# Stick-breaking attention: value products of two units together, projection steps dealt three and one, odd scores in the transposes' banks

## The chip, the core and the metric

The kernel runs on one core of a Trainium2 chip. The time is the device time of one execution, in microseconds (us). The engines work through instruction queues of their own and wait for each other through semaphores: PE does the matmuls (its weight loads are listed apart as PEld), ACT activations and casts, DVE elementwise work and scans, POOL a little elementwise work, SP issues the DMAs. PSUM, into which matmuls write, has eight banks; a tile of 128 x 512 fp32 fills one.

## The reference

A trunk of two layers: a recurrent block, an FFN, a stick-breaking attention and another FFN, on 1024 tokens of 1024 channels. The change is in the attention:

```python
def stick_breaking_attention(x, w_qkv, w_o):
    bsz, seq, _ = x.shape
    qkv = jnp.einsum("bsd,de->bse", x, w_qkv).reshape(bsz, seq, 3, N_HEADS, HEAD_DIM)
...
    scale = 1.0 / math.sqrt(HEAD_DIM)
    outs = []
    for blk in range(seq // Q_BLOCK):
        t0 = blk * Q_BLOCK
        t1 = t0 + Q_BLOCK
        qb = q[:, :, t0:t1]
        kb = k[:, :, :t1]
        vb = v[:, :, :t1]
        z = jnp.einsum("bhqd,bhkd->bhqk", qb, kb).astype(jnp.float32) * scale
...
        strict = s_idx < t_idx
        log_fail = jnp.where(strict, jax.nn.log_sigmoid(-z), 0.0)
        suffix = lax.cumsum(log_fail, axis=3, reverse=True) - log_fail
        weights = jnp.where(strict, jnp.exp(jax.nn.log_sigmoid(z) + suffix), 0.0)
        outs.append(jnp.einsum("bhqk,bhkd->bhqd", weights.astype(vb.dtype), vb))
...
    return jnp.einsum("bse,ed->bsd", o, w_o)
```

There are 16 heads of 64 channels and query blocks of 128.

## The kernel before

Matrices that need fp32 accuracy are kept as a high and a low part, and a product is three matmuls (mm3, L142: high x high, high x low, low x high). Heads are treated in eight pairs, q = 0 to 7, with hx = 0 or 1 for the head within its pair; LAST (L1700) is pair 7.

The attention runs as one loop of steps u, from -10 to 191 (L1915), in an order that is written out by hand (manual_schedule): on each engine the instructions run in the order in which the Python code issues them. A step mixes several streams of work:

- A **score chunk** (chunk_list, L1681). Each head has 12: eight on the diagonal (j = 0 to 7, 256 to 512 keys wide) and four off it (j = 4 to 7, 512 wide). z_part (L1686) does two matmuls into a bank of the pool psZ, which has two banks; z_rest (L1708) is ACT's sigmoid of it into SBUF; scan (L1730) is DVE's scan along the keys. One step later turn_weights (L1742) casts the result to fp16 (ACT), takes the rest (DVE, L1751) and has SP transpose both by DMA into tiles T. Chunks run ten steps ahead of the value products.
- A **unit of value products** (unit_list, L1762). Each head has 12: group G = 0 has key blocks 0 to 3, group G = 1 has 4 to 7 and then 0 to 3. av_part (L1785) does two fp16 matmuls (four for the first two blocks of the diagonal) that add into one bank of psO; with the last block of a group the result goes to ACT and DVE.
- **Projection steps** ("fill", qkv_steps, L1571): each is one mm3 of 512 columns towards q, k and v of the next pair, in psQ (two banks). Eight make a group; after the last one evacuate (L1600) copies the result out in two halves: the first is issued at once, the second when the next projection step is called. The start of a projection also issues the load of raw weights (load_link, L1523) and queues the split of the next weights.
- **Queued pieces**: `later` gives one piece a step (splitting weights, gathering results, the norms' squares and sums, column_norms L1530), `due` runs what was set for this step (copies and transposes of q, k and v by SP and ACT), and one or two loads (`back`) bring stored results back to SBUF.

For the last pair the weights are not turned by DMA: t_part (L1766) transposes them on PE into psT (two banks, used for nothing else) and t_split (L1775) casts and splits them on ACT and DVE; the products of unit u+2 and u+3 are prepared at an even step u. As projections run out, out_fill (L1857) begins the output projection (tiles ob and ob_ps). Before the change each even step calls its own av_part, ahead of the projection steps (or, from the last pair on, ahead of the transposes), and each odd step calls its own at its end; two projection steps follow in each:

```python
                if u % 2 == 0 and 0 <= u < last_two - 2:
                    av_part(*units[u])
...
                if u >= -2:
                    for _ in range(2):
                        next(fill, None)
...
                if u % 2 and u >= 0:
                    av_part(*units[u])
```

In the trace the scores are z_ps, the value products av_ps, the projections qk_ps, the PE transposes wt_ps, the norms' sums n_ps.

Of the kernel before, what the change touches and what calls it, by code (L numbers as in the profile page):

```python
# [8 lines left out]
F32 = mybir.dt.float32  # L9
# [8 lines left out]
P = 128  # L18
# [4 lines left out]
NB = 512  # L23
# [11 lines left out]
def trunk(  # L35
# [166 lines left out]
    def stats(acc, ps_pool, tag, n, i0=0, i1=4):  # L202
        ps = ps_pool.tile([P, NB], F32, tag=tag, name="st_ps")
        accs = acc if isinstance(acc, tuple) else (acc,)
        for i in range(i0, i1):
            for a in accs:
                nc.tensor.matmul(
                    ps[:, i : i + 1], lhsT=a[:, i * P : (i + 1) * P], rhs=ones, start=a is accs[0], stop=a is accs[-1]
                )
        rstd(rcol[:, 4 * n + i0 : 4 * n + i1], ps[:, i0:i1])  # L210
# [49 lines left out]
    with ExitStack() as st, tc.manual_schedule(engines={E.PE, E.Activation, E.DVE, E.Pool, E.SP}):  # L260
# [49 lines left out]
        ps = pst("vps0")  # L310
# [71 lines left out]
        for r0, r1 in ((0, 32), (32, 64), (64, P)):  # L382
            ps = pst("vps")
# [1088 lines left out]
    NP = HEADS // 2  # L1472
# [15 lines left out]
    with ExitStack() as st:  # L1488
# [3 lines left out]
        psZ = pos.enter_context(tc.tile_pool(name="psZ", bufs=2, space=PSUM, side="right", reuse_waits="tile"))  # L1492
        psT = st.enter_context(tc.tile_pool(name="psT", bufs=2, space=PSUM, reuse_waits="tile"))
# [26 lines left out]
        def stage(task, steps=1):  # L1520
            soon.append([steps, task])

        def load_link(i):  # L1523
            q, which = divmod(i, 3)
            if q < NP:
                raws[i] = load_raw(cols(w_qkv, which * D + q * P), (ND,))
            else:
                mix[0].load(which)

        def column_norms(raw, q):  # L1530
            sq = ap.tile([P, ND, P], BF16, tag="vx", name="sq", bufs=2)
            r3 = raw.rearrange("p (k c) -> p k c", k=ND)

            def sums():
                n_ps = psZ.tile([P, NB], F32, tag="z", name="n_ps")[:, 0:1]
                for k in range(ND):
                    nc.tensor.matmul(
                        n_ps, lhsT=sq[:, k], rhs=g2[:, k : k + 1], start=k == 0, stop=k == ND - 1
                    )

                n2, h = (ap.tile([P, 1], t, tag=x, name=x, bufs=2) for x, t in (("n2", F32), ("nh", I32)))
                sv[q], av_[q] = (ap.tile([P, 1], I32, tag=x, name=x, bufs=3) for x in ("sv", "av"))
                nc.vector.tensor_scalar(n2, n_ps, 1e-30, 2.0, op0=ALU.max, op1=ALU.mult)
                one = float(1 << 23)
                nc.vector.tensor_single_scalar(h, n2.bitcast(I32), 24, op=ALU.logical_shift_right)

                def factors():
                    nc.gpsimd.tensor_scalar(sv[q], h, -one, 213 * one, op0=ALU.mult, op1=ALU.add)
                    nc.gpsimd.tensor_scalar(av_[q], h, one, 41 * one, op0=ALU.mult, op1=ALU.add)

                stage(factors, 2)

            squared = lambda i: nc.scalar.square(sq[:, 4 * i : 4 * i + 4], r3[:, 4 * i : 4 * i + 4])
            return lambda: squared(0), lambda: squared(1), sums
# [123 lines left out]

        W = {}

        def chunk_list(q, hx):  # L1681
            cut = lambda j: (j + 1) * P - (NB if j >= 4 else 0)
            diag = [(q, hx, j, j // 4, j // 4 * NB, j // 4 * NB + max(cut(j), 256), True) for j in range(NT)]
            return diag + [(q, hx, j, 0, 0, NB, False) for j in range(4, NT)]

        def z_part(q, hx, j, ci, c0, c1, diag):  # L1686
            nk = (j + 1) * P
            ps = psZ.tile([P, NB], F32, tag="z", name="z_ps")
            lhsT = Q[q][hx][:, j * P : (j + 1) * P]
            nc.tensor.matmul(ps[:, 0 : c1 - c0], lhsT=lhsT, rhs=KK[q][hx][:, 0, c0:c1], start=True, stop=False)  # L1690
            nc.tensor.matmul(ps[:, 0 : c1 - c0], lhsT=lhsT, rhs=KK[q][hx][:, 1, c0:c1], start=False, stop=True)  # L1691
            return ps
# [1 line left out]

        LAST = NP - 1  # L1700

        def stay(key, shape, tag):
            if key not in W:
# [4 lines left out]
        def z_rest(ps, q, hx, j, ci, c0, c1, diag):  # L1708
            n = min(c1, (j + 1) * P) - c0
            if q == LAST:  # L1710
                if not diag:
# [28 lines left out]
        T = {}  # L1740

        def turn_weights(q, hx, j, ci, c0, c1, diag):  # L1742
            paired = diag and j % 4 < 2
            if q == LAST or paired and j % 4 == 0:
                return
# [16 lines left out]
        def unit_list(q, hx):  # L1762
            kbs = ((0, 1, 2, 3), (4, 5, 6, 7, 0, 1, 2, 3))
            return [(q, hx, G, kb, kb == 4 * G, kb == 3) for G in range(2) for kb in kbs[G]]
# [20 lines left out]
        def av_part(q, hx, G, kb, first, last):  # L1785
# [5 lines left out]
            parts_ = []  # L1791
            if q == LAST:
                parts_ = [(q0, NB, t[:, q0:].rearrange("p (j c) -> p j c", c=P)) for t in ready.pop((hx, G, kb))]
# [53 lines left out]
        units = [u for q, hx in heads for u in unit_list(q, hx)]  # L1847
# [27 lines left out]
        with tc.manual_schedule(engines={E.PE, E.Activation, E.DVE, E.Pool, E.SP}):  # L1875


            load_link(1)
            first = qkv_steps(0)
            between = {  # L1880
                12: lambda: stats(rbc[0], psO, "o", 0),
                16: lambda: stats(rbc[1], psO, "o", 1),
                18: lambda: nc.gpsimd.tensor_scalar_mul(rs, rcol, -SC),
                22: lambda: broadcast_r(psO, "o", 0),
                25: lambda: broadcast_r(psO, "o", 1),
            }
            def due():
                now = soon[:]
                soon.clear()
                for steps, task in now:  # L1890
                    if steps > 1:
                        stage(task, steps - 1)
                    else:
                        task()

            for i in range(1, 2 * ND * NH + 3 + AHEAD):
                next(first)
                if i in between:
                    between[i]()
                due()  # L1900
                if i > 4 and later:
                    later.pop(0)()

            gains = [len(units) - x for x in (31, 29, 27)]

            last_two, out_work = len(units) - 2 * 12, out_fill()
            amount = {x: 2 for x in (9, 10, 11, 12)}
            amount.update({x: 1 for x in (*range(-5, 1), *range(14, 21))})
            c = 0

            def turn(some):
                for a in some:
                    turn_weights(*a)

            for u in range(-LEAD, len(units)):  # L1915
                some = chunks[c : c + 1]
                c += 1
                if u < -2:
                    for _ in range(2):
                        next(fill, None)  # L1920
                due()
                for _ in range(2 if u >= last_two - 8 and u % 2 == 0 else 1):
                    if back:
                        nc.sync.dma_start(*back.pop(0))
                for a in some:
                    z_rest(z_part(*a), *a)
                if u % 2 == 0 and u + 2 >= last_two:
                    av_part(*units[u])
                    two = [(x, t_part(*x)) for x in units[u + 2 : u + 4]]
                    for x, tp in two:  # L1930
                        ready[x[1:4]] = t_split(tp, *x)
                for a in some:
                    scan(*a)
                now, turning = turning, list(some)
                turn(now)
                if u % 2 == 0 and 0 <= u < last_two - 2:
                    av_part(*units[u])
                if u - last_two == 9:
                    mix[0].w[mix[0].order[1]] = next_weights(mix[0].raw.pop(1), nc.gpsimd)
                if later:  # L1940
                    later.pop(0)()
                if u >= -2:
                    for _ in range(2):
                        next(fill, None)
                for _ in range(amount.get(u - last_two, 0)):
                    next(out_work)
                if u in gains:
                    z_rest(z_part(*chunks[c]), *chunks[c])
                    scan(*chunks[c])
                    turning.append(chunks[c])  # L1950
                    c += 1
                if u % 2 and u >= 0:
                    av_part(*units[u])
            while later or soon:
                due()
                if later:
                    later.pop(0)()
# [46 lines left out]
```

## Time and profile before

| | us |
|---|---|
| median of 3 runs | 2114.78 (2114.1 to 2115.55) |
| profiled execution, its own time | 2114.74 |
| its span, first to last instruction | 2112.9 |
| first and last start of a score matmul in it | 989.9 and 1374.6 |
| first and last start of a value product | 1006.3 and 1392.4 |

A row of a group names line, engine, operation and tiles (out<-in), then the shape and the count; a row of a timeline gives the start in us, the duration, and in brackets how long the engine was idle before and what released it. Rows of waits read: who waited, for whom, us in all, times, the longest. Matmul records start when the matmul is taken up and their ends are modelled, so that neighbours overlap. PEclk is the share of the full TensorE clock that was granted.

### The profile page before, as it was taken

What the parts mean: (1) busy time and instruction counts of PE and PEld (TensorE: products, weight loads), DVE (VectorE), ACT (ScalarE), POOL (GpSimd) and SP (SyncE); (2) the same over time, 40 slices, a digit from 0 to 9 for tenths busy, and PEclk for the clock granted to TensorE, in tenths of its full rate; (3) what the DMA queues carried; (4) which work ended last, traced back from release to release, by engine and by line L of the source; (5) the groups of instructions that cost most, each with busy time, mean ns of one, the idle gap of its engine ahead of it and who ended that gap; (6) DMA issues with size and microseconds to landing.
All of it is one profiled execution on the core that took longest, in us unless ns stands there. A gap on an engine that the chain in (4) does not pass through costs nothing.

```text
span 2112.9 us, 27977 instructions
## 1 busy us (share of the span) xinstructions
PE 2096.9 (99%) x10022; PEld 1720.7 (81%) x10022; DVE 1771.3 (84%) x2579; ACT 1184.6 (56%) x1906; POOL 139.1 (7%) x118
## 2 busy tenths in 40 slices
PE   8999999999999999999999999999999999999998
PEld 7888888888888888888777777678888888888887
DVE  6888768888888788796999999968888888888886
ACT  6567535444444445466778878744544444454456
POOL 1222010000000000000011111011000000000002
PEclk9999999999999999999999999999999999999999
DMA  7111431334434776434888888952224444686452
GB/s 241 50 45 45 144 105 50 110 120 145 162 129 158 244 256 199 147 118 100 163 176 177 177 175 175 245 170 80 85 90 150 139 150 157 202 269 223 128 153 90
DMA packets 446444, 313.89 MB, mean 149 GB/s; under 512 B 166104, under 2 KB 361824, under 8 KB 446304
## 3 DMA queue, kind: packets, MB, share of 16 engines
q1 hardware_dynamic: 446144, 311.84, 51.5%
q8 instruction: 78, 1.28, 0.3%
q14 instruction: 62, 0.51, 0.1%
q10 hardware_dynamic: 160, 0.27, 0.0%
HBM read 183.57 MB, written 82.84 MB: 126 GB/s over the span
## 4 chain that ended last, share of the span: by engine, by line
PE 97%; DVE 1%; DMA 1%; ACT 1%; issue 0%; SPq 0%; DVEq 0%; ACTq 0%
PE p_ps L143 18%; PE p_ps L145 18%; PE p_ps L144 18%; PE qk_ps L143 4%; PE qk_ps L144 4%; PE qk_ps L145 4%; PE av_ps L1802 3%; PE a_ps L144 3%; PE a_ps L145 3%; PE a_ps L143 3%; PE ob_ps L143 3%; PE ob_ps L144 3%; PE ob_ps L145 3%; PE z_ps L1690 2%; PE z_ps L1691 2%; PE i_ps L145 1%
## 5 line engine op out<-in xcount | busy, mean ns | idle before, releaser
L143 PE MATMUL p_ps<-vh,wbh 128*128 128x512 f32 x524 | 204.9, 391 | 0.0
L144 PE MATMUL p_ps<-vl,wbh 128*128 128x512 f32 x524 | 204.5, 390 | 0.0
L145 PE MATMUL p_ps<-vh,wbl 128*128 128x512 f32 x524 | 204.0, 389 | 0.2 <-DVE wbl L726 0.2
L143 PE MATMUL p_ps<-vh,wch 128*128 128x512 f32 x524 | 204.2, 390 | 0.0
L145 PE MATMUL p_ps<-vh,wcl 128*128 128x512 f32 x524 | 204.1, 390 | 0.0
L144 PE MATMUL p_ps<-vl,wch 128*128 128x512 f32 x524 | 203.9, 389 | 0.0
L722 ACT CAST wbh<-sb 128x1024 fp32r<-128x1024 f32 (+2 forms) x69 | 69.6, 1009 | 192.7 <-DVE sb L702 192.7
L144 PE MATMUL p_ps<-vl,wah 128*128 128x512 f32 x396 | 154.1, 389 | 0.0
L143 PE MATMUL p_ps<-vh,wah 128*128 128x512 f32 x396 | 154.0, 389 | 0.0
L145 PE MATMUL p_ps<-vh,wal 128*128 128x512 f32 x396 | 154.0, 389 | 0.0
L145 PEld LDWEIGHTS p_ps<-vh,wbl 128*128 128x128 f32 x524 | 98.4, 188 | 21.7 <-DVE wbl L726 0.7
L145 PEld LDWEIGHTS p_ps<-vh,wcl 128*128 128x128 f32 x524 | 98.4, 188 | 21.1 <-DVE wcl L736 0.6
L143 PEld LDWEIGHTS p_ps<-vh,wch 128*128 128x128 f32 x524 | 98.3, 188 | 20.4 <-ACT tb L1181 0.2
L144 PEld LDWEIGHTS p_ps<-vl,wch 128*128 128x128 f32 x524 | 98.4, 188 | 20.4
L143 PEld LDWEIGHTS p_ps<-vh,wbh 128*128 128x128 f32 x524 | 98.6, 188 | 19.9 <-ACT U L1181 0.4
L144 PEld LDWEIGHTS p_ps<-vl,wbh 128*128 128x128 f32 x524 | 98.6, 188 | 18.4
L143 PE MATMUL qk_ps<-vh,whi 128*128 128x512 f32 x264 | 112.9, 428 | 0.0
L1728 ACT ACTIVATE w<-z_ps,rs 128x512 f32<-128x512 f32 (+2 forms) x168 | 96.7, 579 | 14.2 <-PE z_ps L1691 11.8
L144 PE MATMUL qk_ps<-vl,whi 128*128 128x512 f32 x264 | 103.6, 392 | 0.0
L145 PE MATMUL qk_ps<-vh,wlo 128*128 128x512 f32 x264 | 103.5, 392 | 0.0
L1750 ACT CAST wx<-w 128x512 f16<-128x512 f32 (+1 forms) x140 | 80.1, 572 | 39.3 <-DVE w L1735 20.4
L1735 DVE TENSOR_TENSOR_SCAN w<-w,unit 128x128 f32<-128x128 f32 (+1 forms) x112 | 93.4, 834 | 9.5 <-ACT w L1728 8.3
(417 smaller groups left out, 5835.6 us busy)
## 6 DMA issues: line engine op xcount, KB each, us to landing
raw<-in_ffn_w_in SPq DMA_DIRECT2D x88, 512.0 KB, 4.0
vl<-pd SPq DMA_DIRECT2D x128, 256.0 KB, 3.7
pd<-U SPq DMA_DIRECT2D x90, 256.0 KB, 2.3
raw<-in_ffn_w_out SPq DMA_DIRECT2D x56, 256.0 KB, 3.8
raw<-in_attn_w_qkv SPq DMA_DIRECT2D x24, 512.0 KB, 4.1
h<-hd SPq DMA_DIRECT2D x32, 256.0 KB, 5.8
hd<-h SPq DMA_DIRECT2D x32, 256.0 KB, 2.0
g<-hd SPq DMA_DIRECT2D x32, 256.0 KB, 5.5
```

The lines of the kernel that those rows point to most:

```text
L143: nc.tensor.matmul(ps, lhsT=wh, rhs=mh, start=first, stop=False, **kw)
L144: nc.tensor.matmul(ps, lhsT=wh, rhs=ml, start=False, stop=False, **kw)
L145: nc.tensor.matmul(ps, lhsT=wl, rhs=mh, start=False, stop=last, **kw)
L722: nc.scalar.copy(self.full(self.wb), self.full(self.sb))
L1690: nc.tensor.matmul(ps[:, 0 : c1 - c0], lhsT=lhsT, rhs=KK[q][hx][:, 0, c0:c1], start=True, stop=False)
L1691: nc.tensor.matmul(ps[:, 0 : c1 - c0], lhsT=lhsT, rhs=KK[q][hx][:, 1, c0:c1], start=False, stop=True)
L1728: nc.scalar.activation(F, ps[:, 0:n], AF.Sigmoid, scale=rs[:, j : j + 1])
L1735: nc.vector.tensor_tensor_scan(rev, rev, unit[:, NB - n :][:, ::-1], 0.0, op0=ALU.mult, op1=ALU.add)
L1750: nc.scalar.copy(wx[:, 0:m, 0], F)
L1802: nc.tensor.matmul(ps[:, c0:c1].rearrange("p (j c) -> p j c", c=P), lhsT=VV[q][:, hx, kb], rhs=t, start=first and i == 0, stop=last and i ...
```

## The change

The norms' sums take a bank of psT in place of psZ. Scores of odd j take a bank of psT, those of even j one of psZ; the last pair's all stay in psZ. The value products of an even step are no longer issued in it, neither in the body nor in the last pair, but at the end of the odd step behind it, just ahead of that step's own. Even steps call three projection steps, odd steps one. LAST is defined further up, with the same value.

```diff
             def sums():
-                n_ps = psZ.tile([P, NB], F32, tag="z", name="n_ps")[:, 0:1]
+                n_ps = psT.tile([P, NB], F32, tag="T", name="n_ps")[:, 0:1]
...
         def z_part(q, hx, j, ci, c0, c1, diag):
             nk = (j + 1) * P
-            ps = psZ.tile([P, NB], F32, tag="z", name="z_ps")
+            pool, tag = (psT, "T") if j % 2 and q < LAST else (psZ, "z")
+            ps = pool.tile([P, NB], F32, tag=tag, name="z_ps")
...
                 if u % 2 == 0 and u + 2 >= last_two:
-                    av_part(*units[u])
                     two = [(x, t_part(*x)) for x in units[u + 2 : u + 4]]
...
-                if u % 2 == 0 and 0 <= u < last_two - 2:
-                    av_part(*units[u])
...
                 if u >= -2:
-                    for _ in range(2):
+                    for _ in range(1 if u % 2 else 3):
                         next(fill, None)
...
                 if u % 2 and u >= 0:
+                    av_part(*units[u - 1])
                     av_part(*units[u])
```

More of the change, by code (lines that the diff above doesn't have):

```diff
@@ L1679, in trunk @@
         W = {}
+        LAST = NP - 1
         def chunk_list(q, hx):
@@ L1692, in z_part @@
             return ps
-        LAST = NP - 1
         def stay(key, shape, tag):
```

## The prediction

> **What bounds the kernel now.** The first view is the page: how busy each engine is over the whole span.
>
> ```profile
> span 2112.9 us, 27977 instructions
> ...
> PE 2096.9 (99%) x10022; PEld 1720.7 (81%) x10022; DVE 1771.3 (84%) x2579; ACT 1184.6 (56%) x1906; POOL 139.1 (7%) x118
> ```
>
> PE is idle for 2112.9 - 2096.9 = 16.0 us in all. The change touches only the attention, so the second view is the busy time by stretch: the body of the attention loop, where projections, scores and value products are mixed, then two stretches of its end, where the last head pair runs without projections.
>
> ```profile
> core 0: us, PE busy (x) PEld busy (x) DVE busy (x) ACT busy (x) POOL busy (x), PEclk, DMA share, GB/s
> 1006.00:1340.00 334.00, 334.00 (x1740) 252.49 (x1739) 319.07 (x459) 271.21 (x503) 35.76 (x46) 1.00 0.87 176
> ...
> 1344.00:1371.00 27.00, 23.28 (x133) 16.19 (x133) 26.79 (x41) 19.18 (x38) 2.89 (x2) 1.00 1.09 280
> 1371.00:1395.00 24.00, 24.00 (x135) 17.80 (x135) 17.93 (x26) 11.12 (x24) 2.57 (x2) 1.00 0.53 188
> ```
>
> In the body PE is never idle (334.00 of 334.00) at full clock, and DVE is close behind: 319.07 of 334.00, so 14.93 us idle. From 1344 to 1371 the order turns round: PE is idle for 27.00 - 23.28 = 3.7 us and DVE for 0.2. After 1371 PE is full again. The third view, what PE waited for over the whole run, says the same.
>
> ```profile
> PE ob L144 <- DMA vl<-odl: 1.5, 1, 1.5
> PE av_ps L1802 <- DVE wx L1780: 1.4, 3, 0.7
> PE z_ps L1690 <- ACT wd L1728: 0.9, 2, 0.7
> PE n_ps L1537 <- ACT sq L1553: 0.2, 1, 0.2
> ```
>
> The first three rows are the attention's, all of them in its end: 3.8 us. A score waits for a bank only twice, for 0.9 us together. So this change has little to remove: 3.8 us of waits, and whatever is hidden between back-to-back matmuls. A busy row cannot show the latter; it is read from start to start in the fourth view, PE's timeline of a few steps of the body.
>
> ```profile
> 1013.81 0.28 PE L1802 MATMUL av_ps<-wd,v 128*128 128x128 f16 x2
> 1013.91 0.42 PE L1690 MATMUL z_ps<-kk,q 128*128 128x384 f32 x1
> 1014.17 0.34 PE L1691 MATMUL z_ps<-kk,q 128*128 128x384 f32 x1
> 1014.35 0.39 PE L1802 MATMUL av_ps<-wp,v 128*128 128x256 f16 x2
> 1014.58 0.38 PE L1802 MATMUL av_ps<-wd,v 128*128 128x256 f16 x2
> 1014.71 0.48 PE L143 MATMUL qk_ps<-vh,whi 128*128 128x512 f32 x1
> 1015.03 0.39 PE L144 MATMUL qk_ps<-vl,whi 128*128 128x512 f32 x1
> 1015.26 0.40 PE L145 MATMUL qk_ps<-vh,wlo 128*128 128x512 f32 x1
> ...
> 1056.19 0.60 PE L1802 MATMUL av_ps<-wt,v 128*128 128x512 f16 x2
> 1056.45 0.58 PE L1690 MATMUL z_ps<-kk,q 128*128 128x512 f32 x1
> 1056.87 0.40 PE L1691 MATMUL z_ps<-kk,q 128*128 128x512 f32 x1
> 1057.10 0.39 PE L1802 MATMUL av_ps<-wp,v 128*128 128x256 f16 x2
> ```
>
> A 512-wide projection matmul takes 1015.26 - 1015.03 = 0.23 us, two 256-wide value products 1014.58 - 1014.35 = 0.23, the second score of 384 columns 1014.35 - 1014.17 = 0.18. The first fp32 matmul behind value products is recorded early and long, so a switch is priced over both.
>
> **The change part by part.**
>
> Value products of even steps move to the end of the odd step (L1925 to L1952). No product is added or removed; 84 of 168 separate runs of fp16 matmuls in the body (14 heads of 12 units) join the run behind them. What goes is a switch from fp32 to fp16 and back, 84 times. Its price: from the first product at 1014.35 to the second projection at 1015.03 are 0.68 us, and the work in it is two pairs of 0.23 and a projection of 0.23, 0.69: nothing extra. Behind 512-wide products: 1056.19 to 1056.87 are 0.68, of which the first score takes as much as the second, 1057.10 - 1056.87 = 0.23, which leaves 0.45 for two 512-wide products, where two at 0.22 (a later row, 1370.94 to 1371.16) need 0.44: 0.01 extra. So, with the rounding, a switch costs between 0 and 0.02 us. I take the middle, 0.01: 84 x 0.01 = **0.8 us gained**, ends 0 and 1.7. The one dear switch is behind a 128-wide pair: from 1013.81 to 1014.17 are 0.36 us, for a first score of 0.18 and two products that cannot take more than half of a 256-wide pair, 0.115: some 0.07 exposed. Such a pair belongs to the last key block of a group (an odd unit), and it still stands last before a score, so this stays.
>
> Three projection steps in even and one in odd steps (L1940): PE's total in a pair of steps is unchanged. An odd step's score now comes after three projection steps in place of two and a run of products: later by 0.69 (three times 0.23) less 0.23 to 0.46 of products, so 0.23 to 0.46 us. That moves work of ACT and DVE, and I cost it at nothing, because the following rows cover it.
>
> ```profile
> DVE w L1735 <- ACT w L1728: 6.4, 14, 1.6
> DVE w L1738 <- ACT w L1728: 5.9, 9, 0.8
> ...
> 1056.56 0.68 DVE L1559 TENSOR_TENSOR wlo<-raw,whi 128x512 fp32r<-128x512 f32 x1
> ...
> 1059.41 0.39 PE L143 MATMUL qk_ps<-vh,whi 128*128 128x512 f32 x1
> ...
> 1059.72 0.59 ACT L1660 CAST two<-qk_ps 128x512 fp32r<-128x512 f32 x1
> ...
> 1064.39 0.69 DVE L1651 TENSOR_TENSOR two<-qk_ps,two 128x512 fp32r<-128x512 f32 x1
> ```
>
> In the whole body DVE waits for a sigmoid only 14 + 9 = 23 times; in the other steps its queue is behind, and a later score finds it still at older work. A late score of an odd step is made good before the next pair begins, as the even step's score stands where it stood. The price without this cover is the second rival's.
>
> A projection group now ends at the second of three steps of an even step, and the third step issues the second half of its evacuation in the same step. For q, DVE's subtraction (L1651) then stands right behind ACT's cast (L1660), and can wait for it: at worst 0.59 us each, 13 times in the body, 7.7 us of DVE's 14.93 idle. In the rows the cast ends at 1060.31 and DVE comes to the subtraction at 1064.39, a step apart in order and 4 us in time, so most of this is covered; behind DVE's wait would stand the next scan and the split of turned weights, which PE needs only steps later. The same shift puts each group's loads and stores on SP (512 KB of raw weights, the copies of q and k, the transposes of v) up to one step earlier, ahead of that step's transposed weights; the first user of each tile of transposed weights is an even unit, whose product now comes later by a score and a projection step, over a microsecond. The weights of the next group are needed up to one projection step earlier within the pair, about 0.7 us; in the rows their low half is done at 1057.24 and the group begins at 1059.41: 2.2 us to spare. Cost nothing.
>
> Odd scores (not those of the last pair) and the norms' sums take the transposes' two banks: scores have four banks where they had two. In the body no score waits (PE idle 0.00), the norms' sums wait 0.2 us once, for ACT's squares and not for a bank. The transposes (L1766) use these banks only at the end, when no score is there any more. Gain and cost nothing.
>
> The end, last pair: at even steps the transposes of the next two units (t_part) no longer stand behind the product of this unit. Here DVE is the limit.
>
> ```profile
> 1364.42 0.28 PE L1691 MATMUL z_ps<-kk,q 128*128 128x256 f32 x1
> 1364.54 0.39 PE L1802 MATMUL av_ps<-wx,v 128*128 128x512 f16 x1
> 1365.24 0.38 PE L1802 MATMUL av_ps<-wx,v 128*128 128x512 f16 x1 [0.32 <-DVE wx L1780]
> ...
> 1370.23 0.39 PE L1802 MATMUL av_ps<-wx,v 128*128 128x512 f16 x1
> 1370.94 0.38 PE L1802 MATMUL av_ps<-wx,v 128*128 128x512 f16 x1 [0.32 <-DVE wx L1780]
> 1371.16 1.04 PE L1770 MATMUL wt_ps<-ident,wt 128*128 128x128 f32 x8
> 1371.96 0.48 PE L1690 MATMUL z_ps<-kk,q 128*128 128x512 f32 x1
> ...
> 1370.24 1.25 DVE L1780 TENSOR_TENSOR wx<-wt_ps,wx 128x512 f16<-128x512 f32 x2
> ```
>
> The product at 1370.94 waits for the first of DVE's two subtractions that begin at 1370.24 (the split of this unit's weights). That subtraction also frees the bank into which the next transposes go. So the wait does not vanish: it moves from the product to the transposes, which then begin at about 1370.9; the last four need the other bank, free at 1370.24 + 1.25 = 1371.49, and take half of 1371.96 - 1371.16 = 0.8: done at 1371.9, as before. But before, PE had by then done this unit's two products (0.22 each by 1371.16 - 1370.94), the first of them inside the wait; now both are still to do. From 1371 PE is full, so what is left over comes out at the end: 0.44 less the 0.07 by which the transposes end sooner, **0.4 us lost**. The earlier waits (a bank, the DMA) lie within the stretch that DVE fills; if they shrink, the waits for DVE grow by as much. Ends: 0.4 gained, if DVE's order lets it split earlier, to 2.2 lost, if each of the five even steps with split weights before 1376 loses 0.44.
>
> The sum, against the profiled execution's own time, 2114.74 us (span 2112.9 and 1.8 around it; the median of the runs is 2114.78): 2114.74 - 0.8 + 0.4 = **2114.3 us**.
>
> **The rivals.**
>
> *The end's waits go.* Products behind split weights get a step more, and loads that are issued a step earlier land in time. If all 3.8 us went and a switch cost 0.02 us: 2114.74 - 3.8 - 1.7 = 2109.2. For it: each such wait is in the profile. Against it: DVE idles 0.2 us of 27 there, and none of its work is taken away. Chance 0.06, half of it past 0.2%.
>
> *PE has room that its busy row hides.*
>
> ```profile
> L143 PEld LDWEIGHTS p_ps<-vh,wbh 128*128 128x128 f32 x524 | 98.6, 188 | 19.9 <-ACT U L1181 0.4
> ...
> L1802 PEld LDWEIGHTS <-v x496: 94/98/102, 1006.3 to 1392.2; 128*128 128x128 f16 x166
> ```
>
> Weight loads fill 252.49 of 334.00 us, 76%. If longer runs let loads fill as much as between two projections, 0.188 of 0.23 us or 82%, the body would take 308 us, 26 less: 2089. Against it: the starts above leave no room between matmuls, and the fp16 loads are short (98 ns beside 188), which lowers the share without leaving PE idle. Chance 0.02. (The Trainium skill, Perfetto Trace Analysis, section Identifying the Most-Contended Engine, says that matmul busy share is a poor measure of the headroom and that the share of weight loads is to be used; by that rule the body would have a quarter of headroom. The trace does not bear it out here, by the starts and the 98 ns just named.)
>
> *Slower: DVE becomes the body's bound.* The place is the scan of the odd step's chunk, the price 0.23 to 0.46 us (0.35 in the middle) for each of 84 pairs of steps, 29 us, against 14.93 us of idle time: 14 us over, 2129. It decides from 14.93 / 84 = 0.18 us lost a pair. For it: DVE at 96%, and evacuations that now wait. Against it: it waits in only 23 steps. Chance 0.14, smaller sizes down to 4 us among it.
>
> **How the numbers follow.** The forecast has the remaining chance, 0.78, with 2112.6 to 2116.9 as its own range: 1.7 and 0.4 gained, to 2.2 lost with nothing gained. A measurement can tell 0.2% from no change, 4.2 us: below 2110.6 is faster, above 2119.0 slower. Faster: 0.03 + 0.02 and a little of the forecast's edge, 0.06. Slower: 0.14. Same: 0.80. The range reaches some way into the rivals: 2111.8 to 2118.
>
> **What would show it.** Right: in the body still no wait of PE, DVE busy within a few us of 319, odd steps with runs of four to eight value products, and the waits for DVE at L1770, with none at L1802. Wrong: a row in which PE waits in the body (for a weight, a tile of transposed weights, a projection's bank), above all for DVE; or a body shorter by more than 2 us, which the switches cannot pay; or an end in which DVE is idle.

## The result: 1.7% slower, and the profile after

| | us |
|---|---|
| before, median of 4 runs beside the changed kernel | 2114.44 |
| after, median of 4 runs | 2150.03 |
| ratio, 95% interval | 1.0171 (1.0159 to 1.0183) |
| profiled execution after: span | 2148.1 |

The forecast was 2114.3, no change. The loss is 35.6 us, 5.1 for each of the seven head pairs whose projections run inside the loop. The page of the changed kernel, and its busy time in the same 334 us of clock time as before (a slower kernel gets through less of its work in them):

```profile
span 2148.1 us, 28006 instructions
...
PE 2108.6 (98%) x10022; PEld 1734.5 (81%) x10022; DVE 1770.4 (82%) x2579; ACT 1187.4 (55%) x1906; POOL 133.0 (6%) x118
```

```profile
core 0: us, PE busy (x) PEld busy (x) DVE busy (x) ACT busy (x) POOL busy (x), PEclk, DMA share, GB/s
...
1006.00:1340.00 334.00, 313.89 (x1583) 241.94 (x1583) 289.08 (x419) 247.12 (x455) 26.25 (x40) 0.96 0.80 159
```

The work of the whole run is the same (10022 matmuls, 2579 DVE instructions), but in this stretch PE, never idle there before, is now idle for 334.00 - 313.89 = 20.1 us, DVE for 44.9 in place of 14.9, and the granted clock is 0.96 in place of 1.00. Over the whole run PE's idle time grew from 16.0 to 2148.1 - 2108.6 = 39.5 us, by 23.5, and its busy time for the same matmuls by 2108.6 - 2096.9 = 11.7 us; together they are the 35.2 us by which the span grew. What PE waited for (who, for whom, us in all, times, the longest):

```profile
PE n_ps L1537 <- ACT sq L1553: 21.4, 8, 3.2
...
PE qk_ps L145 <- DVE wlo L1559: 2.1, 5, 1.1
PE wt_ps L1770 <- DVE wx L1780: 2.1, 4, 0.8
```

Nearly all of the added idle time is one row that read 0.2 before: the norms' sums wait for ACT's squares, up to 3.2 us. The timeline of one such wait:

```profile
1135.67 0.39 PE L1695 MATMUL z_ps<-kk,q 128*128 128x512 f32 x1
1135.90 0.25 PE L1537 MATMUL n_ps<-g,sq 128*128 128x1 bf16 x4
...
1136.39 0.68 DVE L1665 TENSOR_TENSOR two<-qk_ps,rbc 128x512 f32<-128x512 f32 x1
...
1137.11 0.62 ACT L1673 CAST two<-two 128x512 fp32r<-128x512 f32 x1 [1.46 <-DVE two L1665]
1137.63 0.68 ACT L1728 ACTIVATE w<-z_ps,rs 128x512 f32<-128x512 f32 x1
...
1138.35 1.23 DVE L1735 TENSOR_TENSOR_SCAN w<-w,unit 128x512 f32<-128x512 f32 x1 [1.27 <-ACT w L1728]
1138.62 0.63 ACT L1553 ACTIVATE sq<-raw 128x512 bf16<-128x512 f32 x1
...
1139.30 0.27 PE L1537 MATMUL n_ps<-g,sq 128*128 128x1 bf16 x4 [3.15 <-ACT sq L1553]
...
1140.00 0.63 PE L144 MATMUL qk_ps<-vl,whi 128*128 128x512 f32 x1
1140.43 0.63 PE L145 MATMUL qk_ps<-vh,wlo 128*128 128x512 f32 x1
```

The same place before:

```profile
1075.75 0.63 ACT L1553 ACTIVATE sq<-raw 128x512 bf16<-128x512 f32 x1
1076.28 0.68 ACT L1728 ACTIVATE w<-z_ps,rs 128x512 f32<-128x512 f32 x1
...
1076.80 0.68 DVE L1665 TENSOR_TENSOR two<-qk_ps,rbc 128x512 f32<-128x512 f32 x1
...
1077.25 0.63 ACT L1553 ACTIVATE sq<-raw 128x512 bf16<-128x512 f32 x1
...
1077.78 0.61 ACT L1673 CAST two<-two 128x512 fp32r<-128x512 f32 x1
...
1078.20 0.34 PE L1537 MATMUL n_ps<-g,sq 128*128 128x1 bf16 x8
```

In both kernels DVE multiplies the projected k by its norm factor (L1665) and ACT casts the product (L1673). Before, the cast stands behind the second squares, two steps after the product, and does not wait. After, it stands one step after the product, in front of the second squares: ACT reaches it first and waits 1.46 us, then the sigmoid behind it is late, though its score (L1695) was begun at 1135.67 and done by 1136.1, DVE's scan waits 1.27 us for that sigmoid, the squares come last, and the sums, of which the first four have run, wait 3.15 us. The slack was thin all along: the second squares ended at 1077.88 and the sums began at 1078.20.

After the wait PE's matmuls are 0.43 us apart (1140.00 to 1140.43) where they were 0.23. The busy time in and behind the wait, with the granted clock in the third column from the right:

```profile
1136.00:1139.20 3.20, 0.15 (x5) 0.06 (x3) 1.93 (x4) 2.09 (x5) 0.00 (x0) 0.84 0.33 67
1139.20:1142.60 3.40, 3.30 (x12) 2.63 (x13) 2.90 (x5) 3.34 (x7) 0.00 (x0) 0.50 0.83 209
1142.60:1146.00 3.40, 3.40 (x13) 2.29 (x11) 1.38 (x4) 1.65 (x4) 0.49 (x3) 0.64 0.74 152
```

PE stands still, and behind the wait the clock is at half for some 6 us (3.4 at 0.50, and as much of the next 3.4 as makes 0.64). The Trainium skill (TensorE: Matmul & The Clock Gate, section What's actually happening) says that the clock is halved after an idle window of some 3.4 us and comes back after a busy one. The trace agrees on the half clock, but not on the length of the idle time: this wait of 3.15 us is shorter, and the clock had fallen before it ended (0.84 in its row). Nor does the length decide alone: behind the wait that ends at 1084.85, also of 3.15 us, the clock stays at 1.00, and behind one of 2.32 us that ends at 1022.42 it is at half for some 3.4 us.

The other side is what ACT and DVE waited for, in 214 us of the body (1106 to 1320), first before, then after:

```profile
DVE w L1738 <- ACT w L1728: 3.5, 5, 0.8
DVE w L1735 <- ACT w L1728: 3.0, 8, 0.5
...
ACT w L1728 <- PE z_ps L1691: 5.3, 9, 0.8
...
ACT two L1673 <- DVE two L1665: 1.5, 4, 0.4
```

```profile
DVE w L1735 <- ACT w L1728: 19.0, 20, 1.4
DVE w L1738 <- ACT w L1728: 10.1, 13, 2.0
ACT w L1728 <- PE z_ps L1695: 14.3, 19, 1.8
ACT two L1673 <- DVE two L1665: 14.0, 8, 2.0
```

ACT's waits for the product grew from 1.5 to 14.0 us, DVE's for the sigmoids from 6.5 to 29.1. So there are three suspects (the second and third are rivals A and B in the texts below): the place of one cast, the uneven deal as such, and the new banks.

### The profile page after: what moved, and what is told of

Its sections match the earlier page's. It is cut to its first block, busy times and chain, and to the rows that moved or that the text cites. A ratio compares the mean times of both kernels' runs of the same rounds, so it can differ in the third digit from the quotient of the medians.

```text
span 2148.1 us, 28006 instructions
## 1 busy us (share of the span) xinstructions
PE 2108.6 (98%) x10022; PEld 1734.5 (81%) x10022; DVE 1770.4 (82%) x2579; ACT 1187.4 (55%) x1906; POOL 133.0 (6%) x118
## 2 busy tenths in 40 slices
DMA packets 446445, 313.89 MB, mean 146 GB/s; under 512 B 166105, under 2 KB 361825, under 8 KB 446305
## 4 chain that ended last, share of the span: by engine, by line
PE 87%; DVE 6%; ACT 3%; issue 3%; DMA 1%; SPq 0%; DVEq 0%; ACTq 0%
PE p_ps L143 18%; PE p_ps L144 18%; PE p_ps L145 18%; PE a_ps L144 3%; PE a_ps L145 3%; PE a_ps L143 3%; PE ob_ps L145 3%; PE ob_ps L143 3%; PE ob_ps L144 3%; PE qk_ps L143 2%; PE qk_ps L144 2%; PE qk_ps L145 2%; PE av_ps L1802 1%; PE i_ps L145 1%; PE i_ps L144 1%
## 5 line engine op out<-in xcount | busy, mean ns | idle before, releaser
L143 PE MATMUL qk_ps<-vh,whi 128*128 128x512 f32 x264 | 106.7, 404 | 0.0
L143 PE MATMUL p_ps<-vh,wd 128*128 128x512 f32 x254 | 99.4, 391 | 0.0
```

The costliest lines, as they stand in the source:

```text
L143: nc.tensor.matmul(ps, lhsT=wh, rhs=mh, start=first, stop=False, **kw)
```

## The experiments

"Theory" is at first the order of cast and squares.

**The changed kernel with two projection steps in every step.**

```diff
-                    for _ in range(1 if u % 2 else 3):
+                    for _ in range(2):
```

> The changed kernel with two projection steps in every step again; banks and the place of the value products stay as changed. Theory (the cast of k stands in front of the squares on ACT, and PE's norms' sums wait for the squares): with two and two the cast comes a step later again, so PE's waits for the squares fall from 21 us to under 1 us, the clock in the body goes back to 1.00, and the time is 2112 to 2116. Rival A (projection steps dealt three and one bring the odd scores late, and DVE and ACT lose time in every pair of steps): the same time, 2112 to 2116. Rival B (the sums are held up by their new banks): the waits stay, 2145 to 2152.

Measured: 2114.54 us, ratio to before 1.0 (0.9991 to 1.001).

```profile
PE n_ps L1537 <- ACT sq L1553: 1.0, 4, 0.4
```

With two and two, the banks and the moved products cost nothing that can be told; the loss comes with the deal. That leaves the cast and the unevenness.

**The kernel before with the deal alone.**

```diff
-                    for _ in range(2):
+                    for _ in range(1 if u % 2 else 3):
```

> The kernel before with only the projection steps dealt three and one. Theory (cast in front of the squares): the waits are there, each shorter by the 0.45 us of value products that still run ahead of the sums, some 2.7 us seven times, and the clock falls behind each: 2138 to 2150. Rival A (uneven deal): 2145 to 2152, but with lost time spread over the pairs, not in seven places. Rival B (banks): 2112 to 2117.

Measured: 2142.26 us, ratio 1.013 (1.0115 to 1.0145).

```profile
PE n_ps L1537 <- ACT w L1728: 9.9, 7, 1.5
PE n_ps L1537 <- ACT sq L1553: 5.2, 8, 0.8
PE z_ps L1690 <- ACT w L1728: 4.5, 7, 0.8
```

The deal alone makes most of the loss. With the scores' old two banks the sums wait first for a bank, whose sigmoid stands behind the cast, and then for the squares.

**The changed kernel with k's cast one step later.**

```diff
-                stage(high)
+                stage(high, 2 if q else 1)
```

> The changed kernel with one edit: the high cast of k of pairs 1 to 7 is issued one step later, in the step in which the kernel before has it, behind the squares; three and one, banks and products stay as changed. Theory (cast in front of the squares): the waits for the squares fall under 3 us in all, clock 1.00, 2111 to 2117. Rival A (uneven deal): 2140 to 2150. Rival B (banks): 2145 to 2152.

Measured: 2116.97 us, ratio 1.0013 (1.0003 to 1.0022).

```profile
PE n_ps L1537 <- ACT sq L1553: 3.8, 6, 0.7
ACT two L1673 <- DVE two L1665: 1.6, 4, 0.4
```

One argument takes back 33 of 35.6 us, with the uneven deal still in place; ACT's waits for the product, 14.0 us in the 214 of the changed kernel, are back at 1.6. The rest of the waits (expected under 3 us) is longer than in the run with two and two, 3.8 against 1.0.

**The kernel before with k's cast one step earlier, nothing else.**

```diff
                     next(ev)
+                    if which == 1 and q:
+                        next(ev, None)
                     yield
```

> The kernel before with one edit: the second half of k's evacuation is issued in the same step as the first for pairs 1 to 7, so that the cast comes one step earlier, in front of the second squares; projection steps two and two, banks and products as before. Theory (cast in front of the squares): seven waits for the squares of 2 to 3 us each appear in a kernel that has nothing else of the change, and the time is 2132 to 2150. Rival A (uneven deal): 2112 to 2117. Rival B (banks): 2112 to 2117.

Measured: 2139.79 us, ratio 1.0117 (1.01 to 1.0134). First the 334 us of the body, then the waits in the same 214 us (the edit moves the lines below it by two):

```profile
1006.00:1340.00 334.00, 322.54 (x1623) 240.04 (x1621) 300.52 (x427) 251.95 (x467) 35.61 (x43) 0.98 0.81 163
...
DVE w L1737 <- ACT w L1730: 14.9, 16, 1.4
...
ACT two L1675 <- DVE two L1667: 13.8, 8, 2.0
```

The early cast makes a loss of 25 us in a kernel that has nothing else of the change. The waits at the sums were shorter than I expected, 1.6 us each in place of 2 to 3 (6.6 us for a bank and 4.7 for the squares in all), and yet the time was in the range: a first sign that these waits are not the cause but the place where it shows. The 25 us are not free of the clock: behind five of the seven pairs of waits, of some 1.7 us together, it is at half for some 3.4 us, by an estimate 5 x 1.7 = 8.5 us of matmul time.

**The changed kernel with the sums one step later.**

```diff
-                stage(factors, 2)
+                stage(factors, 1 if q else 2)
...
-            return lambda: squared(0), lambda: squared(1), sums
+            return lambda: squared(0), lambda: squared(1), (lambda: stage(sums)) if q else sums
```

> The changed kernel with the norms' sums of pairs 1 to 7 issued one step later, behind three projection steps (the factors that follow one step sooner after them); the cast stays in front of the second squares. Theory (PE waits because the sums stand too close behind squares that the cast has delayed): PE reaches the sums 2.1 us later, so of each wait of 3.2 us some 1 us is left, the clock stays above 0.99, and the time is 2116 to 2127. Rival A (uneven deal): 2145 to 2152.

Measured: 2139.59 us, ratio 1.0117 (1.01 to 1.0134): a miss.

```profile
PE qk_ps L145 <- DVE wlo L1559: 13.7, 6, 2.6
PE n_ps L1537 <- ACT sq L1553: 4.8, 5, 1.3
```

The waits for the squares went as expected, to some 1 us each, and the time fell by 10.4 us, not by the 23 and more that I expected: PE waited 2.3 us a pair for DVE's half of the next weights instead. So PE stands where it next meets ACT or DVE, and 25 us of loss are left.

**The deal mirrored, one and three.**

```diff
-                    for _ in range(1 if u % 2 else 3):
+                    for _ in range(3 if u % 2 else 1):
```

> The changed kernel with the deal mirrored: one projection step in even and three in odd steps. The deal is as uneven as in the change, but a group of eight now ends on the first projection step of an odd step, so that the high cast of k comes in the step in which the kernel before has it. Theory (cast in front of the squares): no wait for the squares over 1 us, 2112 to 2119. Rival A (uneven deal): 2135 to 2152.

Measured: 2141.88 us, ratio 1.0132 (1.0117 to 1.0147): a miss too. The cast stood behind the squares, as before, but ACT waited for the product all the same, and PE for the squares:

```profile
PE n_ps L1537 <- ACT sq L1553: 15.5, 14, 1.9
...
ACT vx L1627 <- DVE t L1612: 16.9, 8, 2.2
ACT two L1673 <- DVE two L1665: 13.6, 8, 2.0
```

Here the group ends on the first projection step of an odd step, so the product itself is a step later than before and the cast again one step behind it. The theory was too narrow: the squares can be late without a cast in front of them. What the early cast in the kernel before, the mirrored deal and the change have in common is the distance, one step from DVE's product to ACT's cast in place of two; the squares' place differs.

**The changed kernel with the sums' bank put back.**

```diff
-                n_ps = psT.tile([P, NB], F32, tag="T", name="n_ps")[:, 0:1]
+                n_ps = psZ.tile([P, NB], F32, tag="z", name="n_ps")[:, 0:1]
```

> The changed kernel with the sums' bank taken from the scores' pool again, the rest as changed. Theory (cast in front of the squares): the bank has no part in the waits; they stay with 21 us in all, and the time is 2147 to 2154. Rival B (the new bank holds the sums up): 2112 to 2120.

Measured: 2150.11 us, ratio 1.0169 (1.0154 to 1.0185), with the same 21.4 us of waits for the squares. The sums' bank has no part in it.

**The changed kernel with useless matmuls in front of the sums.** They go into the bank that the sums overwrite.

```diff
...
+                for k in range(12 if q else 0):
+                    nc.tensor.matmul(n_full, lhsT=unit[:, 0:P], rhs=unit, start=True, stop=True)
                 for k in range(ND):
```

> The changed kernel with twelve useless bf16 matmuls of 512 columns (2.6 us) in front of the norms' sums of pairs 1 to 7, written into the bank that the sums then overwrite: 84 matmuls, 18 us of work more. It separates what the waits cost from what the lower clock behind them costs. If the clock falls because PE stands idle: PE works through most of each wait, 0.6 us of each is left, the granted clock in the body goes from 0.96 to 1.00, and in spite of the added work the time falls by the some 10 us that the slow matmuls cost, to 2137 to 2143. If the clock plays no part: the same time as the changed kernel, 2148 to 2152.

Measured: 2139.03 us, ratio 1.0117 (1.0101 to 1.0132).

```profile
1006.00:1340.00 334.00, 328.18 (x1703) 248.84 (x1702) 297.05 (x429) 252.29 (x466) 33.77 (x43) 1.00 0.82 164
```

Some 18 us of useless work make the changed kernel 11.0 us faster (2150.03 - 2139.03): the clock is 1.00 again, and ACT's waits for scores in the 214 us are 5.5 us in place of 14.3. DVE is still idle for 36.9 us of 334. So of the 35.6 us, some 11 are the clock's, which fits the 11.7 us by which PE's busy time had grown; some 25 stay with the clock at 1.00. The 11 are a net figure, as part of the useless work may stand in PE's way.

From here on the theory is the refined one: distance, not order.

**The mirrored deal with the cast one step later** (the edits of the mirrored deal and of the later cast).

> The mirrored deal (one projection step in even, three in odd steps) with the high cast of k of pairs 1 to 7 one step later. Theory, refined (the loss is the step between DVE's product L1665 and ACT's cast L1673: with one step between them ACT waits 1.5 to 2 us, the sigmoids behind it are late, DVE idles and becomes the bound; the mirrored deal also had one step, the kernel before two): ACT's waits for L1665 fall from 14 us in 214 to under 3, DVE's idle time with them, and the time is 2112 to 2119. Older theory (order of cast and squares): the cast stood behind the squares already, so no change, 2138 to 2145. Rival A (uneven deal): 2138 to 2145.

Measured: 2122.83 us, ratio 1.0038 (1.0025 to 1.0052).

```profile
PE n_ps L1537 <- ACT sq L1553: 7.7, 7, 1.3
...
ACT vx L1627 <- DVE t L1612: 16.9, 8, 2.2
...
ACT two L1673 <- DVE two L1665: 1.3, 4, 0.3
```

ACT's waits for the product fell from 13.6 to 1.3 us and the time by 19 us, but it is 4 above the range. PE lost the rest in front of the norms' sums: its idle time is 7.8 us above that of the kernel before, and 7.5 of that is the first row. V's cast (L1627) also still waits 16.9 us for its subtraction, 6.4 in the kernel before, though by the code it stands two steps behind it, as before: the count of steps alone does not say how long ACT waits.

**The kernel before with v's cast one step earlier.**

```diff
-                stage(high, 3 if (q, n) == (NP - 1, 1) else 2)
+                stage(high, 3 if (q, n) == (NP - 1, 1) else 1 if q else 2)
```

> The kernel before with one edit at another place: the cast of v on ACT (L1627) stands one step behind DVE's subtraction (L1612) in place of two, pairs 1 to 7; the squares come in other steps. Theory, refined (distance of a cast to its DVE producer): ACT's waits for L1612 grow by 1 to 2 us each, fourteen times, DVE idles more than the 1.6 us a pair that it has to spare, and the time is 2120 to 2142. Older theory (order of cast and squares): 2112 to 2117. Rival A (uneven deal): 2112 to 2117.

Measured: 2130.88 us, ratio 1.0077 (1.0062 to 1.0092).

```profile
ACT vx L1627 <- DVE t L1612: 25.7, 8, 3.3
...
PE z_ps L1690 <- ACT w L1728: 11.6, 12, 1.4
```

The same cut at another cast does the same: ACT's waits for v grow from 6.4 to 25.7 us, and PE meets the delay at the scores' two banks, where no wait was before. The sums hardly wait for the squares here (0.2 us), so the first theory falls and the refined one holds. The clock stays at 1.00 in the body here, so these 16 us are lost without it.

**The changed kernel with k's early cast on DVE.**

```diff
-                    nc.scalar.copy(two[:, 0], t)
+                    (nc.vector.tensor_copy if q else nc.scalar.copy)(two[:, 0], t)
```

> The changed kernel with k's high cast of pairs 1 to 7 taken from ACT to DVE, in the same early step; fourteen casts of some 0.6 us of work more for DVE and less for ACT. Theory, refined: ACT no longer waits for L1665, so the sigmoids come in time; DVE has 1.2 us a pair more to do and 1.6 to spare: 2113 to 2125, clock 0.99 or more. Rival A (uneven deal): 2145 or more, since DVE has more work and the same late scores.

Measured: 2118.26 us, ratio 1.0018 (1.0009 to 1.0028). DVE, the fuller of the two engines, does more work, and the kernel is 32 us faster than the change: on DVE the cast follows its product in the same queue and does not wait for ACT. ACT's copies of the result (L1640) wait 5.1 us for it in the 214 us.

**The changed kernel with the cast and the sums one step later** (the edits of the later cast and of the later sums).

> The changed kernel with two repairs: k's high cast one step later (two steps behind its product, as before) and the norms' sums one step later, behind three projection steps. With the cast alone repaired PE still waited 3.8 us for the squares. Theory, refined: that goes too, and the time is 2111 to 2116, no more than 3 us below the kernel before, since PE has no other wait in the body. Rival A (uneven deal): 2115 to 2120, DVE idle above that of the kernel before.

Measured: 2115.97 us, ratio 1.0007 (0.9998 to 1.0017).

```profile
1006.00:1340.00 334.00, 333.94 (x1749) 258.63 (x1748) 314.04 (x458) 270.83 (x502) 36.23 (x46) 1.00 0.88 177
```

PE is full again in the body (333.94 of 334.00), and the time is that of the kernel before, within what can be told. No version that I tried beats the kernel before: its body had nothing to give.

## Why the prediction was wrong

**The step that failed** is the shift of the evacuation. The prediction saw that a projection group now issues the second half of its evacuation in the same step, and wrote "Cost nothing". It priced q's half, where DVE would wait 0.59 us for ACT, and did not look at k's, where ACT waits for DVE. There the half that moves sets the date of the cast, which stood two steps behind DVE's product and came to stand one behind it. In the prediction's rows DVE came to q's subtraction 4 us after ACT's cast; such a lag of DVE was taken as cover (a late score finds DVE at older work), and it is what makes k's cast wait: ACT comes to it while DVE is still at older work.

**The price.** The kernel before with the early cast alone shows 25 us, with a share of the lower clock in it; the later cast in the changed kernel takes 33 back, waits and clock together. ACT and DVE work in order and feed each other, sigmoid to scan, scan to cast: a wait of ACT delays the sigmoids behind it, and DVE stands still for them. DVE's idle time in the 334 us went from 14.9 to 36.9 in the run with the filler, where the clock is 1.00. (The Trainium skill, TensorE: Matmul & The Clock Gate, section Architectural detail, calls ACT and DVE strict first-in, first-out; the timeline agrees, with the ready sigmoid at 1137.63 held behind the waiting cast.) Some 11 us of the 35.6 are the clock behind PE's waits, a term that the prediction did not have; the filler shows it.

**The norms' sums** were costed at nothing because they waited 0.2 us once. A wait of nothing is not a slack of much: it was 0.3 us, and the row of waits can't show that. But they are not the cause: with the sums later 25 of the 35.6 us were still lost.

**The slower rival** named the right engine, DVE, and gave 2129, but the wrong place. It held the late odd scores responsible, 0.35 us in each of 84 pairs of steps; with the uneven deal in place, and k's cast and the sums a step later, nothing is lost that can be told (2115.97). Its threshold, that time is lost once DVE loses more than it has to spare, no run tested by itself.

**What held.** Paired products and new banks change nothing: with two and two, both in place, the time is 2114.54, where the sum said 2114.3; that 0.8 us were gained at the switches and 0.4 lost at the end is below what these runs can tell. The waits of the end moved from the products to the transposes, as forecast (in the run with two and two the transposes, L1770, wait for DVE's splits three times, 1.3 us; before, the products did, 1.4). In the body of the changed kernel no bank held PE up; at the end a score waited 1.1 us for one, 0.9 before.

What stays open: why the mirrored deal with the later cast is 8 us slower than before. PE loses the time in front of the norms' sums, and v's cast waits 16.9 us; but near the one such wait that I followed, at 1131.19, no v cast stands (the nearest ones that waited are at 1100.65 and 1143.79). No run moved the sums or v's cast in that kernel, so the cause is not shown.

## What to carry to other kernels

Where two in-order engines feed each other, an edit that reorders the work of a third has to be followed to every instruction whose distance to its producer on the other engine it changes; one step of distance was worth 25 us here, the clock's share included, and the list of waits before did not show that it was needed. Compute for each such pair by how much the producer is early, not only whether anybody waits. And where an edit makes PE stand still, look at the clock behind the gap: here it fell behind gaps of 1.7 to 3.2 us, though not behind every one, and a few useless matmuls in the gap were cheaper than the gap.

## What the runs showed of the hardware

That seven waits of up to 3.2 us cost some 11 us beyond themselves, through the clock that falls to half behind most of them, and that useless matmuls in the gap take this back, was not in my picture. Nor was it that waits of 1.0 and 0.7 us close together are enough for it (the kernel before with the early cast alone). The granted clock before was 1.00 throughout the attention, so nothing in the profile of before pointed to it.
